# Forgetting attention with its query tiles in reverse order, the causal mask added to the key terms by GpSimd

## The chip, the cores and the metric

The kernel runs on one core of a Trainium2 chip. The metric is the device time of one execution in microseconds; lower is better. The engines are named TensorE (PE in the profile, its weight loads PEld), VectorE (DVE), ScalarE (ACT), GpSimd (POOL) and SyncE (SP).

## The reference, cut to what matters

Two transformer layers run one after the other over 1024 tokens (1040 with 16 meta tokens ahead). The first has a state-space part and a forgetting attention of 16 heads; the second has two more kinds of attention. Only the forgetting attention is touched:

```python
c = jnp.cumsum(logf, axis=1)                       # c: one value per token and head
...
s = jnp.einsum("bthd,bshd->bhts", qi, k).astype(jnp.float32) * scale
s = s + (cqi[..., :, None] - c_k[..., None, :])
s = jnp.where(kpos[None, :] <= qpos[:, None], s, -jnp.inf)
p = jax.nn.softmax(s, axis=-1).astype(v.dtype)
return jnp.einsum("bhts,bshd->bthd", p, v)
```

The term of the query in a row is the same for all keys and drops out of the softmax. The term of the key, and the mask, stay.

## The kernel before, in words

All instructions stand in the order in which the program issues them, and each engine works through its own in that order. The 16 heads go as eight pairs (p = 0 to 7; j = 0, 1 within a pair). For a pair, `fox_project` has made keys, queries and values in an earlier stretch, and `fox_attend` does the attention in eight query tiles of 128 rows, t = 0 to 7. The keys of tile t are the 16 meta columns and 128 (t + 1) more.

For each tile there are three steps. A: TensorE multiplies queries by keys (L566, L567: two products, since the operands are split in two parts), in one to three chunks of columns; the last chunk gets a third product (L569) of an identity with a table of 0 and 1e30 in bf16, which puts the mask into its last 128 columns. VectorE adds the key terms `cb`, takes the minimum (L570) and writes N. ScalarE takes the exponential in place (L573). GpSimd copies the 16 meta columns into `pm` (L576). B: TensorE transposes N in blocks of 128 columns (L624), up to four blocks to a PSUM bank, and ScalarE copies each bank to `pt` (L630). C: after every fourth tile, TensorE multiplies the group's transposed weights with the values (L604, and L607 for the meta columns), and VectorE scales the result (L609). The first group has tiles 0 to 3, the second tiles 4 to 7.

`pipeline` sets their order: A(0), A(1), then A(i + 2), C(i - 1), B(i) for each i. A, B and C return an estimate of their time, and `merge` weaves these steps with projections by such estimates: first with the gate's projection of this pair (two pieces of 24 products, L112 to L114, `fox_gate`), then, from the `None` that `pipeline` yields ahead of the last two tiles' transposes, with the projections for the next pair (keys in three pieces, then queries, then values). In the last pair these are strips of the convolution. When the gate's pieces are used up, attention goes on alone until that `None`. A key piece is taken out of PSUM by ScalarE and VectorE in turn, twice (`stack_q`, L443 and L444).

PSUM has eight banks of 512 columns, handed out in turn (`bank`); a product waits until the bank of eight ago has been read. Weights for projections are loaded by SyncE's queue and split in two by ScalarE (L120) and GpSimd (L121).

Of the kernel before, what the change touches and what calls it, by code (L numbers as in the profile page):

```python
# [9 lines left out]
F32 = mybir.dt.float32  # L10
F32R = mybir.dt.float32r
BF16 = mybir.dt.bfloat16
I32 = mybir.dt.int32
AF = mybir.ActivationFunctionType
ALU = mybir.AluOpType
# [51 lines left out]
class Kern:  # L67
# [128 lines left out]
    def consts(self):  # L196
        nc, V, cst = self.nc, self.nc.vector, self.cst
        self.w32 = cst.tile([128, 32], F32, name="w32")
        V.memset(self.w32, 0.0)
        V.memset(self.w32[0:64, 0:1], 1.0)  # L200
        V.memset(self.w32[64:128, 1:2], 1.0)
        V.memset(self.w32[:, 2:3], 1.0)
        self.identb = cst.tile([128, 128], BF16, name="identb")
        self.maskb = cst.tile([128, 128], BF16, name="maskb")
        V.tensor_copy(out=self.identb, in_=self.ident)
        V.tensor_copy(out=self.maskb, in_=self.cm[:, 3, :])
        self.ones = cst.tile([128, 128], F32, name="ones")
        V.memset(self.ones, 1.0)
        a, b = PARAM_COLS["conv_w"]
        self.cwh = cst.tile([128, 120], F32, name="cwh")  # L210
        V.tensor_scalar(out=self.cwh, in0=self.params[:, a:a + 120], scalar1=0.5, scalar2=None, op0=ALU.mult)
        self.gbh = cst.tile([128, 16], F32, name="gbh")
        V.tensor_scalar(out=self.gbh, in0=self.pslot("gate_bias"), scalar1=0.5, scalar2=None, op0=ALU.mult)
        self.sb48 = cst.tile([48, 1], F32, name="sb48")
        V.tensor_tensor(out=self.sb48, in0=self.pslot("b48")[:48], in1=self.pslot("sgn")[:48], op=ALU.mult)
# [322 lines left out]
    def fox_attend(self, p, st):  # L538
        nc, te = self.nc, self.nc.tensor
        cb = []  # L540
        for j in range(2):
            c = self.ph.tile([128, L], F32, tag="cb", name="cb", bufs=2)
            nc.sync.dma_start(out=c, in_=self.d_csp[2 * p + j].partition_broadcast(128))
            cb.append(c)
        vT = st.pop("vT")
        st["vm"] = self.v_meta(vT)
        st["v"] = self.v_tokens(vT, [16 + 128 * b for b in range(8)])
        y = self.slot("y", w=T)
        Ns, PTs, M = {}, {}, [None, None]

        def A(i):
            if i % 4 == 0:
                M[i // 4] = self.ph.tile([128, 2, 128], F32, tag="bt", name="pm", bufs=2)
            W = 16 + 128 * (i + 1)
            n = -(-W // 512)
            w = -(-W // (2 * n)) * 2
            Ns[i] = []
            for j in range(2):
                N = self.slot("N")
                mn = self.sm.tile([128, 3], F32, tag="mn", name="mn", bufs=4)  # L560
                qt = st["q"][j][:, i * 128:(i + 1) * 128]
                for c in range(n):
                    s0, s1 = c * w, min(W, c * w + w)
                    S = self.bank()[:, :s1 - s0]
                    last = c == n - 1
                    te.matmul(S, qt, st["k"][j][0][:, s0:s1], start=True, stop=False)  # L566
                    te.matmul(S, qt, st["k"][j][1][:, s0:s1], start=False, stop=not last)  # L567
                    if last:
                        te.matmul(S[:, s1 - s0 - 128:], self.identb, self.maskb, start=False, stop=True)  # L569
                    nc.vector.tensor_tensor_reduce(  # L570
                        out=N[:, s0:s1], in0=cb[j][:, s0:s1], in1=S, scale=1.0,
                        scalar=mn[:, c - 1:c] if c else HUGE, op0=ALU.add, op1=ALU.min, accum_out=mn[:, c:c + 1])
                nc.scalar.activation(out=N[:, :W], in_=N[:, :W], func=AF.Exp, scale=-1.0, bias=mn[:, n - 1:n],  # L573
                                     accum_out=self.lall[:, 2 * p + j, i:i + 1])
                c = 32 * (i % 4) + 16 * j
                nc.gpsimd.tensor_copy(out=M[i // 4][:, 0, c:c + 16], in_=N[:, 0:16])  # L576
                Ns[i].append(N)
            return 4 * max(W, 512) / 2.4

        def B(i):  # L580
            if i % 4 == 3:
                ps = self.bank()
                te.transpose(ps[:, :128], M[i // 4][:, 0], self.ident)
                nc.vector.tensor_copy(out=M[i // 4][:, 1], in_=ps[:, :128])
            if i % 4 == 0:

                PTs[i // 4] = [[self.ph.tile([128, 4, 512], F32, tag="pt", name="pt", bufs=4) for _ in range(2)]
                               for _ in range(i // 4 + 1)]
            q = slice((i % 4) * 128, (i % 4 + 1) * 128)
            for j in range(2):  # L590
                self.transposes(Ns[i][j], 16, i + 1, [pt[j][:, :, q] for pt in PTs[i // 4]], act=True)
            del Ns[i]
            return 2 * (i + 1) * 109

        def C(i):
            if i % 4 != 3:
                return 0
            g = i // 4
            pt = PTs.pop(g)
            O = self.bank()  # L600
            for b in range(i + 1):
                c0 = max(0, b - 4 * g) * 128
                for j in range(2):
                    te.matmul(O[64 * j:64 * j + 64, c0:], st["v"][:, b, 64 * j:64 * j + 64],  # L604
                              pt[b // 4][j][:, b % 4, c0:], start=b == 0, stop=False)
            for t in range(4):
                te.matmul(O[:, t * 128:(t + 1) * 128], st["vm"][:, t], M[g][:, 1], start=False, stop=t == 3)  # L607
            c = slice((i - 3) * 128, (i + 1) * 128)
            nc.vector.scalar_tensor_tensor(out=y[:, c], in0=O, scalar=0.5, in1=st["zs"][:, c], op0=ALU.mult,  # L609
                                           op1=ALU.mult)  # L610
            return (2.5 + 4 * g) * 910

        yield from self.pipeline(8, A, B, C)
        nc.sync.dma_start(out=self.d_yatt[p], in_=y)

# [1198 lines left out]
```

## Time and profile before

| | |
|---|---|
| time, median of 3 runs | 2726.68 us (2726.24 to 2726.96) |
| time of the profiled execution | 2726.84 us |
| span in the profile | 2725.1 us |
| busy share of the span: TensorE, VectorE, ScalarE, GpSimd | 98%, 49%, 43%, 27% |
| attention stage touched by the change | from 76 to some 670 us, eight pairs |

The span is the stretch of one execution that the profiler saw; times in the trace count from its start. A busy share is an average over many stages. Matmuls are pipelined and their ends are modelled, so the spacing from start to start says what a product costs, not its duration.

### The profile page before, as it was taken

The numbers are of one execution on the slowest core, as the hardware profiler recorded it, in microseconds if no ns is written. First come the engines' busy times: TensorE is split into PE (matmuls) and PEld (weight loads), VectorE is DVE, ScalarE is ACT, GpSimd is POOL, SyncE is SP. The second block draws the span as 40 slices with busy tenths as digits, with TensorE's granted clock in tenths as the row PEclk, the third lists the DMA queues.
The fourth block names the chain that finished last, engine by engine and source line by source line (L and its number), as shares of the span: only waits on it lengthen the run. The fifth ranks groups of instructions, "written<-read, shape, count | busy, mean of one in ns | idle before, by whom it ended". The sixth has DMA issues, their size and how long they took to land. (4 is left out here: it accounts for less than half of the span.)

```text
span 2725.1 us, 38660 instructions
## 1 busy us (share of the span) xinstructions
PE 2658.2 (98%) x14925; PEld 2229.8 (82%) x14925; DVE 1332.5 (49%) x2625; ACT 1165.5 (43%) x2080; POOL 729.7 (27%) x924
## 2 busy tenths in 40 slices
PE   8999999999999999999999999999999999998999
PEld 6888888888989889889877887878878877787877
DVE  5433322233574573654756777444644454346332
ACT  5554444444443433433432113445544454445331
POOL 1112122111253342342432334111121222225321
PEclk9999999999999999999999999999999999999999
DMA  3222222221123123122168654340222223325412
GB/s 126 64 61 75 78 74 75 78 58 68 39 87 116 55 78 115 55 92 103 55 192 282 207 174 149 108 134 23 85 63 78 79 74 107 95 72 155 155 62 70
DMA packets 85463, 266.86 MB, mean 98 GB/s; under 512 B 10880, under 2 KB 12032, under 8 KB 84256
## 3 DMA queue, kind: packets, MB, share of 16 engines
q1 hardware_dynamic: 81936, 255.68, 28.7%
q10 hardware_dynamic: 3344, 8.72, 1.5%
q8 instruction: 117, 1.92, 0.3%
q14 instruction: 66, 0.54, 0.1%
HBM read 205.57 MB, written 33.49 MB: 88 GB/s over the span
## 5 line engine op out<-in xcount | busy, mean ns | idle before, releaser
L121 POOL TENSOR_TENSOR wlo<-wraw,whi 128x1024 fp32r<-128x1024 f32 (+2 forms) x168 | 376.7, 2246 | 1064.9 <-ACT whi L120 857.6
L112 PE MATMUL bank<-uh,whi 128*128 128x512 f32 (+4 forms) x1752 | 626.6, 358 | 0.1
L114 PE MATMUL bank<-uh,wlo 128*128 128x512 f32 (+4 forms) x1752 | 619.3, 353 | 0.7 <-POOL wlo L121 0.7
L113 PE MATMUL bank<-ul,whi 128*128 128x512 f32 (+4 forms) x1752 | 619.2, 353 | 0.0
L114 PEld LDWEIGHTS bank<-uh,wlo 128*128 128x128 f32 (+1 forms) x1752 | 328.2, 187 | 36.1 <-POOL wlo L121 1.1
L112 PEld LDWEIGHTS bank<-uh,whi 128*128 128x128 f32 (+1 forms) x1752 | 328.5, 188 | 34.2 <-issue 1.1
L113 PEld LDWEIGHTS bank<-ul,whi 128*128 128x128 f32 (+1 forms) x1752 | 328.5, 187 | 32.3
L112 PE MATMUL bank<-u,whi 128*128 128x512 f32 x512 | 208.0, 406 | 0.7 <-ACT pr L935 0.7
L113 PE MATMUL bank<-u,whi 128*128 128x512 f32 x512 | 203.6, 398 | 0.0
L114 PE MATMUL bank<-u,wlo 128*128 128x512 f32 x512 | 203.2, 397 | 0.0
L120 ACT ACTIVATE whi<-wraw 128x1024 fp32r<-128x1024 f32 (+2 forms) x169 | 155.1, 926 | 17.8 <-DMA wraw<-in_w_pa_dram 13.8
L630 ACT ACTIVATE pt<-bank 128x512 f32<-128x512 f32 (+1 forms) x320 | 142.2, 508 | 40.7 <-PE bank L624 37.8
L114 PE MATMUL bank<-yh,wlo 128*128 128x512 f32 x384 | 153.1, 399 | 2.0 <-POOL wlo L121 1.8
L112 PE MATMUL bank<-yh,whi 128*128 128x512 f32 x384 | 152.9, 398 | 1.2 <-ACT whi L120 1.2
L113 PE MATMUL bank<-yl,whi 128*128 128x512 f32 x384 | 152.2, 396 | 0.0
L647 DVE SCALAR_TENSOR_TENSOR acc<-raw,cwh,acc 128x1040 f32<-128x1040 f32 x72 | 93.7, 1302 | 109.5 <-ACT acc L644 107.8
L573 ACT ACTIVATE N<-N,mn 128x272 f32<-128x272 f32 (+7 forms) x128 | 100.3, 786 | 45.6 <-DVE mn L570 44.7
L121 POOL TENSOR_TENSOR wo<-wl,wo 128x512 fp32r<-128x512 f32 x52 | 74.0, 1436 | 158.2 <-ACT wo L120 151.3
L114 PEld LDWEIGHTS bank<-u,wlo 128*128 128x128 f32 x512 | 97.4, 190 | 23.2
L112 PEld LDWEIGHTS bank<-u,whi 128*128 128x128 f32 x512 | 97.6, 191 | 22.2 <-ACT pr L935 1.1
L113 PEld LDWEIGHTS bank<-u,whi 128*128 128x128 f32 x512 | 97.6, 191 | 20.6
L624 PE MATMUL bank<-cm,N 128*128 128x128 f32 x832 | 106.9, 273 | 0.0
(326 smaller groups left out, 4954.6 us busy)
## 6 DMA issues: line engine op xcount, KB each, us to landing
wraw<-in_w_in_dram SPq DMA_DIRECT2D x120, 512.0 KB, 4.0
gt<-d_gate SPq DMA_DIRECT2D x48, 512.0 KB, 4.6
ab<-d_acs SPq DMA_DIRECT2D x32, 512.0 KB, 3.7
qs<-qt SPq DMA_DIRECT2D x48, 256.0 KB, 3.0
wl<-in_w_out_dram SPq DMA_DIRECT2D x48, 256.0 KB, 5.3
tab<-in_tab_dram SPq DMA_DIRECT2D x8, 1056.0 KB, 5.3
cb<-d_csp SPq DMA_DIRECT2D x16, 520.0 KB, 7.7
d_gate<-gt SPq DMA_DIRECT2D x16, 512.0 KB, 2.9
```

Source lines behind the costliest of these rows:

```text
L112: te.matmul(ps, lh, rh, start=start, stop=False)
L113: te.matmul(ps, lh, rl, start=False, stop=False)
L114: te.matmul(ps, ll, rh, start=False, stop=stop)
L120: self.nc.scalar.activation(out=hi, in_=src, func=AF.Copy)
L121: (self.nc.vector if vector else self.nc.gpsimd).tensor_tensor(out=lo, in0=src, in1=hi.bitcast(F32), op=ALU.subtract)
L573: nc.scalar.activation(out=N[:, :W], in_=N[:, :W], func=AF.Exp, scale=-1.0, bias=mn[:, n - 1:n], accum_out=self.lall[:, 2 * p + j, i:i + 1])
L624: nc.tensor.transpose(ps[:, b * 128:(b + 1) * 128], N[:, c:c + 128], self.ident)
L630: self.nc.scalar.activation(out=out, in_=ps, func=AF.Copy)
L647: V.scalar_tensor_tensor(out=acc[:, :L], in0=raw[:, k:k + L], scalar=w(k), in1=acc[:, :L], op0=ALU.mult, op1=ALU.add)
```

## The change

The mask product and its two bf16 tables go. The tile order is reversed: i still counts 0 to 7, and the tile is t = 7 - i. Before the first tile and after each tile's reduction, GpSimd adds the mask in place into the 128 columns of `cb` that lie on the diagonal of the next tile. Smaller tiles never read those columns, so each block of `cb` is masked once, when its tile is next. GpSimd's copies of the meta columns move behind both heads' exponentials. The groups come in the order tiles 7 to 4, then tiles 3 to 0.

```diff
-        self.identb = cst.tile([128, 128], BF16, name="identb")
-        self.maskb = cst.tile([128, 128], BF16, name="maskb")
-        V.tensor_copy(out=self.identb, in_=self.ident)
-        V.tensor_copy(out=self.maskb, in_=self.cm[:, 3, :])
...
+        def mask(j, t):
+            c = cb[j][:, 16 + 128 * t:144 + 128 * t]
+            nc.gpsimd.tensor_tensor(out=c, in0=c, in1=self.cm[:, 3], op=ALU.add)
+
+        mask(0, 7)
+        mask(1, 7)
+
         def A(i):
+            t = 7 - i
...
-                    te.matmul(S, qt, st["k"][j][1][:, s0:s1], start=False, stop=not last)
-                    if last:
-                        te.matmul(S[:, s1 - s0 - 128:], self.identb, self.maskb, start=False, stop=True)
+                    te.matmul(S, qt, st["k"][j][1][:, s0:s1], start=False, stop=True)
                     nc.vector.tensor_tensor_reduce(
                         out=N[:, s0:s1], in0=cb[j][:, s0:s1], in1=S, scale=1.0,
                         scalar=mn[:, c - 1:c] if c else HUGE, op0=ALU.add, op1=ALU.min, accum_out=mn[:, c:c + 1])
+                if t:
+                    mask(j, t - 1)
                 nc.scalar.activation(out=N[:, :W], in_=N[:, :W], func=AF.Exp, scale=-1.0, bias=mn[:, n - 1:n],
-                                     accum_out=self.lall[:, 2 * p + j, i:i + 1])
-                c = 32 * (i % 4) + 16 * j
-                nc.gpsimd.tensor_copy(out=M[i // 4][:, 0, c:c + 16], in_=N[:, 0:16])
+                                     accum_out=self.lall[:, 2 * p + j, t:t + 1])
                 Ns[i].append(N)
+            for j in range(2):
+                c = 32 * (t % 4) + 16 * j
+                nc.gpsimd.tensor_copy(out=M[t // 4][:, 0, c:c + 16], in_=Ns[i][j][:, 0:16])
             return 4 * max(W, 512) / 2.4
...
-            return 2 * (i + 1) * 109
+            return 2 * (t + 1) * 109
...
         def C(i):
             if i % 4 != 3:
                 return 0
-            g = i // 4
+            g = (7 - i) // 4
```

In the new numbering the score products are L571 and L572, the reduction L573, the exponential L578, the mask L551, the meta copy L583, the transposes L632, their copies L638, and the group's products L612 and L615. The order of three places in the fourth pair shows what moves.

On TensorE, the score products of tile 3 (528 key columns, two chunks of 264 for each head), before:

```order
L566 MATMUL bank<-kx_2621,qs_2771 128x264
L567 MATMUL bank<-ky_2622,qs_2771 128x264
L566 MATMUL bank<-kx_2621,qs_2771 128x264
L567 MATMUL bank<-ky_2622,qs_2771 128x264
L569 LDWEIGHTS identb
L569 MATMUL bank<-maskb,identb 128x128
L566 MATMUL bank<-kx_2623,qs_2773 128x264
```

The same place now, with the transposes of tile 5 behind it (12 blocks):

```order
L571 MATMUL bank<-kx_2657,qs_2789 128x264
L572 MATMUL bank<-ky_2658,qs_2789 128x264
L571 MATMUL bank<-kx_2657,qs_2789 128x264
L572 MATMUL bank<-ky_2658,qs_2789 128x264
L571 MATMUL bank<-kx_2659,qs_2791 128x264
L572 MATMUL bank<-ky_2660,qs_2791 128x264
L571 MATMUL bank<-kx_2659,qs_2791 128x264
L572 MATMUL bank<-ky_2660,qs_2791 128x264
L632 MATMUL bank<-cm,N_3077 128x128 x6
L632 MATMUL bank<-cm,N_3089 128x128 x6
```

The mask and its weight load are gone, so the second head's products follow the first head's directly.

On ScalarE, from the gate's second piece (its tanh, L519) to the first group's last copies, before:

```order
L519 ACTIVATE zs_3003<-bank 128x512
L630 ACTIVATE pt<-bank 128x2x128 x2
L573 ACTIVATE N_3143,lall<-N_3143,mn 128x656
L573 ACTIVATE N_3156,lall<-N_3156,mn 128x656
L630 ACTIVATE pt<-bank 128x3x128 x2
L573 ACTIVATE N_3179,lall<-N_3179,mn 128x784
L573 ACTIVATE N_3192,lall<-N_3192,mn 128x784
L630 ACTIVATE pt<-bank 128x4x128 x2
```

The same stretch now (its tanh is L515):

```order
L515 ACTIVATE zs_3017<-bank 128x512
L638 ACTIVATE pt<-bank 128x4x128 x4
L578 ACTIVATE N_3158,lall<-N_3158,mn 128x656
L578 ACTIVATE N_3170,lall<-N_3170,mn 128x656
...
L638 ACTIVATE pt<-bank 128x2x128
L578 ACTIVATE N_3253,lall<-N_3253,mn 128x400
L578 ACTIVATE N_3261,lall<-N_3261,mn 128x400
L638 ACTIVATE pt<-bank 128x4x128
L638 ACTIVATE pt<-bank 128x128
L638 ACTIVATE pt<-bank 128x4x128
L638 ACTIVATE pt<-bank 128x128
```

Between the gate's tanh and the first group's last copy there were two tiles' exponentials and the copies of three tiles; now there are three tiles' exponentials and the copies of four tiles, and these are the large ones.

On TensorE, around the second group's product, now (`vtok` are the values; L632 are the transposes of tiles 1 and 0, L591 that of the meta columns):

```order
L114 MATMUL bank<-uh_8_95,wlo_3019 128x348
L632 MATMUL bank<-cm,N_3292 128x128 x2
L632 MATMUL bank<-cm,N_3300 128x128 x2
L591 MATMUL bank<-cm,pm 128x128
L632 MATMUL bank<-cm,N_3346 128x128
L632 MATMUL bank<-cm,N_3353 128x128
L612 MATMUL bank<-pt,vtok_2966 64x512 x2
```

Before, a whole projection piece stood between the last tile's transposes and the second group's product, and another between the last two tiles' transposes; now the second group, which is the small one, follows its last transposes directly.

## Rows read from the trace of the kernel before

**Rows 1.** The page's first part: busy time, share of the span and instructions.
```profile
PE 2658.2 (98%) x14925; PEld 2229.8 (82%) x14925; DVE 1332.5 (49%) x2625; ACT 1165.5 (43%) x2080; POOL 729.7 (27%) x924
```

**Rows 2.** TensorE's waits from 60 to 690 us: total, times, longest, in us.
```profile
PE bank L604 <- ACT pt L630: 5.6, 8, 0.8
```

**Rows 3.** Windows of the fourth pair: length, then each engine's busy time and count.
```profile
309.95:386.60 76.65, 75.89 (x466) 64.62 (x464) 23.09 (x72) 35.61 (x80) 14.42 (x29) 1.00 0.24 69
324.89:341.04 16.15, 15.39 (x111) 12.79 (x109) 10.50 (x36) 10.70 (x24) 1.18 (x6) 1.00 0.09 32
316.21:319.26 3.05, 3.05 (x26) 2.48 (x24) 2.16 (x8) 1.68 (x6) 0.20 (x1) 1.00 0.01 3
325.24:326.73 1.49, 1.49 (x13) 1.27 (x12) 1.02 (x2) 0.99 (x3) 0.00 (x0) 1.00 0.00 0
```

**Rows 4.** Timeline of TensorE at two masks: start, duration, line and operation.
```profile
318.61 0.23 PE L569 MATMUL bank<-maskb,identb 128*128 128x128 bf16 x1
318.65 0.37 PE L566 MATMUL bank<-kx,qs 128*128 128x264 f32 x1
318.86 0.28 PE L567 MATMUL bank<-ky,qs 128*128 128x264 f32 x1
318.98 0.28 PE L566 MATMUL bank<-kx,qs 128*128 128x264 f32 x1
319.09 0.28 PE L567 MATMUL bank<-ky,qs 128*128 128x264 f32 x1
...
326.67 0.23 PE L569 MATMUL bank<-maskb,identb 128*128 128x128 bf16 x1
326.73 0.83 PE L624 MATMUL bank<-cm,N 128*128 128x128 f32 x6
```

**Rows 5.** Timeline of TensorE at eight transposes and at the first group's product.
```profile
329.13 1.04 PE L624 MATMUL bank<-cm,N 128*128 128x128 f32 x8
329.96 0.47 PE L566 MATMUL bank<-kx,qs 128*128 128x456 f32 x1
...
332.83 2.86 PE L604 MATMUL bank<-pt,vtok 128*64 128x512 f32 x16 [0.76 <-ACT pt L630]
```

**Rows 6.** Timeline of ScalarE in the same stretch.
```profile
319.21 0.61 ACT L573 ACTIVATE N<-N,mn 128x400 f32<-128x400 f32 x1
...
320.75 0.73 ACT L573 ACTIVATE N<-N,mn 128x528 f32<-128x528 f32 x1
...
325.08 0.60 ACT L519 ACTIVATE zs<-bank 128x512 f32<-128x512 f32 x1 [2.68 <-PE bank L114]
325.58 0.66 ACT L630 ACTIVATE pt<-bank 128x256 f32<-128x256 f32 x2
327.62 0.85 ACT L573 ACTIVATE N<-N,mn 128x656 f32<-128x656 f32 x1 [1.39 <-DVE mn L570]
...
328.75 0.84 ACT L573 ACTIVATE N<-N,mn 128x656 f32<-128x656 f32 x1 [0.18 <-DVE mn L570]
...
329.59 0.85 ACT L630 ACTIVATE pt<-bank 128x384 f32<-128x384 f32 x2
...
332.20 1.07 ACT L630 ACTIVATE pt<-bank 128x512 f32<-128x512 f32 x2
333.15 1.06 ACT L573 ACTIVATE N<-N,mn 128x912 f32<-128x912 f32 x1
```

**Rows 7.** Timeline of TensorE and ScalarE behind the second key piece.
```profile
348.80 0.93 PE L624 MATMUL bank<-cm,N 128*128 128x128 f32 x7
...
349.00 0.45 ACT L443 ACTIVATE kx<-bank 64x348 fp32r<-64x348 f32 x1 [1.52 <-PE bank L114]
350.03 0.46 ACT L443 ACTIVATE kx<-bank 64x348 fp32r<-64x348 f32 x1 [0.58 <-DVE ky L444]
350.51 1.85 ACT L630 ACTIVATE pt<-bank 128x512 f32<-128x512 f32 x4
```

**Rows 8.** A GpSimd group (busy, mean ns, idle before), and VectorE at a pair's start.
```profile
L761 POOL TENSOR_TENSOR yq<-yq,th 128x128 f32<-128x128 f32 x128 | 60.7, 506 | 126.5 <-DVE yq L758 126.5
...
311.35 0.30 DVE L570 CUSTOM_DVE_ANT_0 N<-cb,bank 128x144 f32<-128x144 f32 x1 [0.54 <-DMA cb<-d_csp]
```

More of the change, by code (lines that the diff above doesn't have):

```diff
@@ L549, in fox_attend @@
         Ns, PTs, M = {}, {}, [None, None]
+        def mask(j, t):
[3 more added lines that the diff above has]
+        mask(1, 7)
         def A(i):
+            t = 7 - i
             if i % 4 == 0:
-                M[i // 4] = self.ph.tile([128, 2, 128], F32, tag="bt", name="pm", bufs=2)
-            W = 16 + 128 * (i + 1)
+                M[t // 4] = self.ph.tile([128, 2, 128], F32, tag="bt", name="pm", bufs=2)
+            W = 16 + 128 * (t + 1)
             n = -(-W // 512)
@@ L560, in A @@
                 mn = self.sm.tile([128, 3], F32, tag="mn", name="mn", bufs=4)
-                qt = st["q"][j][:, i * 128:(i + 1) * 128]
+                qt = st["q"][j][:, t * 128:(t + 1) * 128]
                 for c in range(n):
@@ L564, in A @@
                     S = self.bank()[:, :s1 - s0]
-                    last = c == n - 1
                     te.matmul(S, qt, st["k"][j][0][:, s0:s1], start=True, stop=False)
-                    te.matmul(S, qt, st["k"][j][1][:, s0:s1], start=False, stop=not last)
-                    if last:
-                        te.matmul(S[:, s1 - s0 - 128:], self.identb, self.maskb, start=False, stop=True)
+                    te.matmul(S, qt, st["k"][j][1][:, s0:s1], start=False, stop=True)
                     nc.vector.tensor_tensor_reduce(
@@ L572, in A @@
                         scalar=mn[:, c - 1:c] if c else HUGE, op0=ALU.add, op1=ALU.min, accum_out=mn[:, c:c + 1])
+                if t:
+                    mask(j, t - 1)
                 nc.scalar.activation(out=N[:, :W], in_=N[:, :W], func=AF.Exp, scale=-1.0, bias=mn[:, n - 1:n],
-                                     accum_out=self.lall[:, 2 * p + j, i:i + 1])
-                c = 32 * (i % 4) + 16 * j
-                nc.gpsimd.tensor_copy(out=M[i // 4][:, 0, c:c + 16], in_=N[:, 0:16])
+                                     accum_out=self.lall[:, 2 * p + j, t:t + 1])
                 Ns[i].append(N)
+            for j in range(2):
+                c = 32 * (t % 4) + 16 * j
+                nc.gpsimd.tensor_copy(out=M[t // 4][:, 0, c:c + 16], in_=Ns[i][j][:, 0:16])
             return 4 * max(W, 512) / 2.4
         def B(i):
+            t = 7 - i
+            g = t // 4
             if i % 4 == 3:
                 ps = self.bank()
-                te.transpose(ps[:, :128], M[i // 4][:, 0], self.ident)
-                nc.vector.tensor_copy(out=M[i // 4][:, 1], in_=ps[:, :128])
+                te.transpose(ps[:, :128], M[g][:, 0], self.ident)
+                nc.vector.tensor_copy(out=M[g][:, 1], in_=ps[:, :128])
             if i % 4 == 0:
-                PTs[i // 4] = [[self.ph.tile([128, 4, 512], F32, tag="pt", name="pt", bufs=4) for _ in range(2)]
-                               for _ in range(i // 4 + 1)]
-            q = slice((i % 4) * 128, (i % 4 + 1) * 128)
+                PTs[g] = [[self.ph.tile([128, 4, 512], F32, tag="pt", name="pt", bufs=4) for _ in range(2)]
+                          for _ in range(g + 1)]
+            q = slice((t % 4) * 128, (t % 4 + 1) * 128)
             for j in range(2):
-                self.transposes(Ns[i][j], 16, i + 1, [pt[j][:, :, q] for pt in PTs[i // 4]], act=True)
+                self.transposes(Ns[i][j], 16, t + 1, [pt[j][:, :, q] for pt in PTs[g]], act=True)
             del Ns[i]
-            return 2 * (i + 1) * 109
+            return 2 * (t + 1) * 109
         def C(i):
@@ L597, in C @@
                 return 0
-            g = i // 4
+            g = (7 - i) // 4
             pt = PTs.pop(g)
             O = self.bank()
-            for b in range(i + 1):
+            for b in range(4 * g + 4):
                 c0 = max(0, b - 4 * g) * 128
@@ L607, in C @@
                 te.matmul(O[:, t * 128:(t + 1) * 128], st["vm"][:, t], M[g][:, 1], start=False, stop=t == 3)
-            c = slice((i - 3) * 128, (i + 1) * 128)
+            c = slice(512 * g, 512 * g + 512)
             nc.vector.scalar_tensor_tensor(out=y[:, c], in0=O, scalar=0.5, in1=st["zs"][:, c], op0=ALU.mult,
```

## The prediction

> **What bounds the kernel now.** The page comes first: TensorE is busy for 98% of the span, so a change pays only through TensorE's own work or through its waits [rows 1]. The table of waits of the attention stage (its eight head pairs) has one entry that matters: products of weights and values (L604) wait 5.6 us in eight pieces for ScalarE's copies of transposed weights [rows 2]. The windows view takes one pair: TensorE is busy 75.89 of 76.65 us, ScalarE 35.61, GpSimd 14.42 [rows 3]. The 0.76 us left over is that one wait [rows 5]. The other row is what to watch: in the 16.15 us in which TensorE does attention work alone, with no projection between, ScalarE is busy 10.70 us, two thirds of the time, where it is under half busy over the pair [rows 3]. So the question is what the new order puts into that stretch.
>
> **Mask products removed.** All 128 go (16 in each pair). TensorE's timeline gives the price from start to start [rows 4]: the next product starts 0.04 us after the mask, but then takes 0.21 us until its successor starts, where the same shape without a mask ahead takes 0.11 to 0.13. So a mask followed by a product of that format costs 0.04 + 0.09 = 0.13 us. One followed by transposes costs 0.06 (326.67 to 326.73). In each pair 11 are of the first sort (the eight of j = 0 and three of j = 1) and 5 of the second: 11 x 0.13 + 5 x 0.06 = 1.73 us, 13.8 us for eight pairs. The same 0.09 us is paid at each change from transposes or group products back to a projection; the order has four of these in a pair before and two now: 2 x 0.09 x 8 = 1.4 us more. Gain: 15.2 us. Its bounds: 0.04 x 128 = 5 us, if the slow successor is not the mask's doing, and 0.13 x 128 + 1.4 = 18 us; I stay near the upper end, since the successor is slow in each row behind a mask and in none behind its own kind. The two casts at the start of the program go too; they lie on VectorE, and I count nothing for them (below 1 us).
> The Trainium skill (TensorE: Matmul & The Clock Gate, Back-to-back issue gap) gives about 81 ns for a product of 128 columns with its weight load in a sustained stream. By that figure 128 masks would be 10.4 us, and the forecast 3 us later; the rows' spacing is used here.
>
> **The masks on GpSimd.** 128 additions of 128x128 are new; the same operation and shape stands elsewhere in the program at 506 ns [rows 8]. That is 8.1 us more in a pair, on an engine busy 14.42 of 76.65. Each is issued right after the reduction of the tile before, and VectorE needs it only for the last columns of the next tile, after another tile's transposes. Ahead of it in GpSimd's queue stand the 16-column copies of a tile whose exponentials are done by then. At a pair's start the key terms' transfer lands late (VectorE waits 0.54 us for it now [rows 8]) and two masks follow it; the gate's projection covers that, some 5.6 us on TensorE (its second piece lies from 319.26 to 324.89 in the windows [rows 3]). I take zero. If the covers fail, the price is 0.5 us for each mask that ScalarE then waits for.
>
> **The first group's wait.** The order of the query tiles decides what is left when the gate's projection has run out. Before, that stretch begins with the third small tile's transposes; now it begins with the largest. I add up both engines from the end of the gate's second piece (t = 0) to the first group's product.
> TensorE: the transposes of tiles 7, 6, 5, 4 are 16 + 14 + 12 + 10 at 0.83/8 = 0.104 us [rows 5], 5.4 us, with one for the meta columns 5.5. The score products of tiles 1, 2, 3 and 4 take 3.05 + 1.49 us in the trace [rows 3]; without the two transposes among them (0.2) and their eight masks (4 x 0.13 + 4 x 0.06), and with the one change of format more, they come to 3.7. TensorE could start at 9.2 us.
> ScalarE, whose queue is in program order, must first do [rows 6]: the gate's tanh (done 0.7 us after the piece ends, 325.08 + 0.5 against the transposes' start at 324.89 us); four copies of 512 columns (0.48 each: from 332.20 to 333.15 for two): 2.6 us. Then tile 4's exponentials (656 wide): its products start at 1.7, and in the trace the exponential comes 2.4 us after them, of which VectorE spent some 0.4 on the gate; with 2.0 it starts at 3.7, and the second is 1.1 us later and 0.84 long: 5.6 us. Then tile 6's copies (2 x (0.48 + 0.37)): 7.3; tile 3's exponentials (2 x 0.73): 8.8; tile 5's copies (2 x (0.48 + 0.28), the tail of 0.12 of a pair's last one taken off): 10.3; tile 2's exponentials (2 x 0.61): 11.5; tile 4's copies up to the second head's first (0.48, half of 0.28, 0.48): 12.6 us, and about 0.1 until it has landed.
> So TensorE is held from 9.2 to 12.7, less some 0.5 us for the first head's product, which needs only the first copy: 3.0 us in place of 0.76 [rows 5]. PSUM's eight banks spread this wait over transposes and scores of the stretch, which doesn't change its sum. Cost: 8 x 2.2 = 17.6 us. Bounds of the wait: 1.7 us, if tile 4's exponentials need not be waited for, and 4.0, if masks hold VectorE back (a rival below).
>
> **The second group's wait.** Before, the order had a whole projection piece between its tiles' last transposes and its product. Now tile 1's and tile 0's transposes stand directly ahead of it. The piece before them ends at the transposes' start, 348.80 us in the trace; ScalarE takes the key copies first, the second of them only after VectorE's part of the first, and comes to the transposes' copies at 350.51, 1.7 us later [rows 7]. Copies of 256, 256 and 128 columns bring it to 2.5 us for the first head; TensorE has done its seven transposes at 7 x 0.104 = 0.73. Wait: 1.8 us in seven pairs. In the eighth the piece is a convolution strip's with a single copy: 0.7. Sum 13.3 us; before, zero. Bounds: 0.8 us a pair, if the second key copy went ahead of its wait, and 1.9.
> What is late next: nothing. Only projections follow in each pair, and their weights are split earlier; TensorE runs through them unheld now.
>
> **The sum.** -15.2 + 17.6 + 13.3 = +15.7 us. The profiled execution took 2726.84 us (span 2725.1), 0.16 above the median of the three runs, 2726.68. Forecast: 2742 us, 0.6% slower.
>
> **Rivals.** What a measurement of this kernel can tell from no change is about 0.2%: 2721.2 to 2732.1 us.
> (1) ScalarE keeps pace, faster. If its queue reached the last copy by 10 us in place of 12.7, the first wait would stay 0.76, and with the second one absent too the time is 2726.8 - 15.2 = 2712 us. For it: over the pair ScalarE is not half busy [rows 3]. Against it: the durations in the stretch are rows, and before the change the wait was there with a lighter queue. It decides from the point where both waits together are under 0.76 + 15.2/8 = 2.7 us in a pair; I add up 4.8. Chance 0.12.
> (2) Only one of the waits appears. With the first alone, 17.6 - 15.2 = +2: 2729 us. With the second alone, 13.3 - 15.2 = -2: 2725 us. For it: TensorE's queue may take up a short wait as slack; the 1.8 us rests on a single spacing. Against it: in-order copies leave nothing to start on. No measurable change. Chance 0.16.
> (3) The masks hold VectorE. Each addition on GpSimd delays the reduction beside it by 0.5 us; two of these are ahead of tile 4's second exponential, for which ScalarE idles anyway: 1.0 us a pair, +8: 2750 us. For it: both engines work on the same key terms. Against it: later delays are hidden, as ScalarE has a backlog from there on. Chance 0.12.
> The Trainium skill (SBUF — State Buffer, Who interferes with whom) says that VectorE is held by a GpSimd instruction that reads SBUF when it has two SBUF inputs, and not with one at most; this reduction reads key terms from SBUF and scores from PSUM, so by that rule (3) would not come from the memory's port. No row here shows it either way.
> (4) The forecast, both waits as summed: 0.60.
>
> **How the numbers follow.** Slower by over 0.2% holds (4), (3) and a little of (2): 0.74. Same holds most of (2): 0.15. Faster is (1) less its edge: 0.11. The range must leave out at most 2 in 10: below, it takes in the first-wait case of (2) at 2729 and stops ahead of (1); above, it takes in (3) with the second wait at its bound, 2756. So 2728 to 2756; for (4) alone 2733 to 2751.
>
> **What would show it.** Right: no L569; TensorE's busy time in the stage down by some 15 us; waits of the group products for ScalarE's copies up from 5.6 us to over 25, in two places of each pair; a pair's period up from 76.65 to some 78.6 us; ScalarE without a gap from tile 4's exponentials to tile 4's copies; GpSimd some 60 us busier with nobody waiting for it. Wrong: waits of VectorE for GpSimd's masks, a period under 76, or group products that start without a wait.

## The result and the profile after

The changed kernel took 2748.63 us (median of five runs, 2744.37 to 2752.05) beside 2726.68 us of the kernel before on the same chip: ratio 1.0082, 95% interval 1.0068 to 1.0096, so 0.8% slower. The forecast was 2742 us within 2728 to 2756. The profiled execution took 2744.37 us (span 2742.3), 17.5 us above that of before (2726.84), where the sum said 15.7.

The page of the changed kernel, part 1:

```profile
PE 2649.9 (97%) x14797; PEld 2241.7 (82%) x14797; DVE 1335.5 (49%) x2623; ACT 1168.3 (43%) x2080; POOL 784.7 (29%) x1052
```

TensorE has 128 products fewer and is busy 8.3 us less than in [rows 1]; GpSimd is busy 55 us more. So TensorE does less and ends later: it waits. The table of its waits from 60 to 700 us answers to [rows 2] (waiting line, what it waits for: total, times, longest):

```profile
PE bank L612 <- ACT pt L638: 26.8, 16, 1.9
PE bank L571 <- DVE zs L516: 2.2, 1, 2.2
PE bank L632 <- DVE mn L573: 1.5, 8, 0.4
...
PE bank L112 <- DVE mn L573: 1.1, 1, 1.1
```

The wait of the group products for ScalarE's copies has gone from 5.6 us in eight pieces to 26.8 in sixteen, two in each pair. Below it stand eight short waits of transposes for VectorE, one in each pair, and two single ones in the first pair, none of which the prediction had. The first pair had one such wait before the change as well, which [rows 2] does not show:

```profile
PE bank L566 <- DVE mn L570: 1.4, 1, 1.4
```

The windows view takes each pair from its first transpose of the values to the next pair's. Here are the first, second and fourth pair, with two stretches of the first pair behind them (length, busy time and count of TensorE, its weight loads, VectorE, ScalarE and GpSimd, then the granted clock, as a share of 2.4 GHz, and the DMA):

```profile
76.59:162.91 86.32, 79.28 (x454) 68.85 (x453) 30.97 (x87) 36.27 (x82) 21.80 (x46) 0.96 0.26 78
162.91:242.72 79.81, 75.98 (x456) 67.02 (x455) 23.44 (x72) 36.83 (x81) 21.02 (x45) 1.00 0.22 64
321.62:400.41 78.79, 75.01 (x448) 66.33 (x447) 23.35 (x72) 35.88 (x79) 21.35 (x45) 1.00 0.24 67
88.00:92.00 4.00, 1.02 (x2) 0.50 (x2) 2.75 (x4) 1.34 (x3) 2.44 (x2) 0.75 0.00 0
92.00:96.00 4.00, 3.88 (x9) 3.14 (x10) 3.48 (x13) 2.56 (x5) 1.45 (x5) 0.50 0.00 0
```

Before, the same three pairs are 79.13, 77.45 and 76.62 us long. The fourth pair, which stands for the steady state, has grown by 2.17 us: TensorE is busy 0.9 us less than in [rows 3] and idle 3.78 us in place of 0.76. The first pair has grown by 7.2 us, and in it the granted clock falls to the lower level, 1.2 GHz (0.50 from 92 to 96 us), after 4 us in which TensorE was busy for 1.02. From the eighth pair to the end the profiled run is 3.9 us shorter than that of before, most of which is not the change's: the run of before had a stretch at the lower clock near 1440 us, up to 3.4 us of work (0.79, 0.50 and 0.86 in three windows of 4 us from 1436 us), and this one has none there. The other four runs are 4 to 8 us longer than the profiled one; their mean granted clocks are 0.993 to 0.995, and 0.996 in the profiled one. An experiment below shows a place where the clock falls.

TensorE's timeline in the fourth pair at the two group products, with the start of the stretch (338.55) and of the last transposes (367.58):

```profile
338.55 1.91 PE L632 MATMUL bank<-cm,N 128*128 128x128 f32 x16
...
348.44 0.28 PE L572 MATMUL bank<-ky,qs 128*128 128x272 f32 x1
350.59 6.45 PE L612 MATMUL bank<-pt,vtok 128*64 128x512 f32 x32 [1.87 <-ACT pt L638]
356.98 1.16 PE L615 MATMUL bank<-pm,vm 128*128 128x128 f32 x8
...
367.58 0.60 PE L632 MATMUL bank<-cm,N 128*128 128x128 f32 x4
...
370.18 2.54 PE L612 MATMUL bank<-pt,vtok 128*64 128x512 f32 x16 [1.67 <-ACT pt L638]
```

ScalarE's timeline in the same stretch:

```profile
338.75 0.60 ACT L515 ACTIVATE zs<-bank 128x512 f32<-128x512 f32 x1 [0.81 <-PE bank L114]
339.24 2.06 ACT L638 ACTIVATE pt<-bank 128x512 f32<-128x512 f32 x4
342.07 0.84 ACT L578 ACTIVATE N<-N,mn 128x656 f32<-128x656 f32 x1 [0.77 <-DVE mn L573]
...
343.23 0.85 ACT L578 ACTIVATE N<-N,mn 128x656 f32<-128x656 f32 x1 [0.22 <-DVE mn L573]
...
344.07 1.82 ACT L638 ACTIVATE pt<-bank 128x512 f32<-128x512 f32 x4
...
349.91 1.45 ACT L638 ACTIVATE pt<-bank 128x512 f32<-128x512 f32 x4
```

Read against the prediction's clock, which starts where the gate's piece ends (338.55): tile 4's exponentials start at 3.5 (forecast 3.7), tile 4's copies at 11.4 (11.5), the first group's product at 12.0 (12.2). From 344.07 on ScalarE has no recorded gap. In the second group the product starts 2.6 us after the last transposes begin (2.5).

The first pair, on all engines (the softplus chain of the state-space part, L334 to L337, is VectorE's work from before; L120 splits a weight):

```profile
77.67 3.57 DVE L334 SCALAR_TENSOR_TENSOR dt<-dt,dt 128x288 f32<-128x288 f32 x7
...
82.58 0.51 DVE L573 CUSTOM_DVE_ANT_0 N<-cb,bank 128x348 f32<-128x348 f32 x1
...
87.70 1.04 ACT L120 ACTIVATE whi<-wraw 128x1024 fp32r<-128x1024 f32 x1
...
88.64 0.57 ACT L515 ACTIVATE zs<-bank 128x512 f32<-128x512 f32 x1
...
89.25 0.69 DVE L516 SCALAR_TENSOR_TENSOR zs<-zs,bank 128x512 f32<-128x512 f32 x1 [2.75 <-ACT zs L515]
...
90.00 0.70 PE L571 MATMUL bank<-kx,qs 128*128 128x392 f32 x1 [2.17 <-DVE zs L516]
...
92.12 0.80 PE L112 MATMUL bank<-uh,whi 128*128 128x512 f32 x1 [1.10 <-DVE mn L573]
```

Tile 7's scores stand from 77.38 us, but VectorE is at its chain until 82.58. Then six reductions follow (before, two short ones stood there), so the exponentials are late, the gate's tanh behind them is late, VectorE waits 2.75 us for the tanh, and the last scores of tile 5 (two chunks of 392 columns for each head) start 2.17 us late, as no bank of PSUM is free.

### The profile page after: what moved, and what is told of

Same layout as the page of the kernel before. It is cut to its first block, busy times and chain, and to the rows that moved or that the text cites. A ratio compares the mean times of both kernels' runs of the same rounds, so it can differ in the third digit from the quotient of the medians.

```text
span 2742.3 us, 38458 instructions
## 1 busy us (share of the span) xinstructions
PE 2649.9 (97%) x14797; PEld 2241.7 (82%) x14797; DVE 1335.5 (49%) x2623; ACT 1168.3 (43%) x2080; POOL 784.7 (29%) x1052
## 5 line engine op out<-in xcount | busy, mean ns | idle before, releaser
L638 ACT ACTIVATE pt<-bank 128x512 f32<-128x512 f32 (+1 forms) x320 | 142.0, 517 | 76.2 <-PE bank L632 73.4
L120 ACT ACTIVATE whi<-wraw 128x1024 fp32r<-128x1024 f32 (+2 forms) x169 | 154.9, 924 | 27.5 <-DMA wraw<-in_w_pa_dram 14.3
L578 ACT ACTIVATE N<-N,mn 128x912 f32<-128x912 f32 (+7 forms) x128 | 101.6, 806 | 54.4 <-DVE mn L573 53.5
L632 PE MATMUL bank<-cm,N 128*128 128x128 f32 x832 | 111.1, 275 | 2.2 <-DVE mn L573 1.5
```

What stands on the lines that cost most here:

```text
L120: self.nc.scalar.activation(out=hi, in_=src, func=AF.Copy)
L632: nc.tensor.transpose(ps[:, b * 128:(b + 1) * 128], N[:, c:c + 128], self.ident)
L638: self.nc.scalar.activation(out=out, in_=ps, func=AF.Copy)
```

## The experiments

All medians against the kernel before on the same chip, with the length of the first and the fourth pair (from values to values, from each profile) and the granted clock of the runs:

| run | us | ratio, 95% interval | first pair | fourth pair | clock |
|---|---|---|---|---|---|
| before | 2726.68 to 2728.38 | | 79.13 | 76.62 | 0.994 to 0.997 |
| changed | 2748.63 | 1.0082, 1.0068 to 1.0096 | 86.32 | 78.79 | 0.993 to 0.996 |
| order alone | 2753.56 | 1.0092, 1.0079 to 1.0105 | 83.86 | 79.72 | 0.993 to 0.997 |
| forward, no mask | 2723.52 | 0.9986, 0.9977 to 0.9995 | 78.97 | 76.04 | 0.994 to 0.996 |
| reverse, no mask | 2750.30 | 1.0078, 1.0066 to 1.0090 | 85.96 | 78.80 | 0.993 to 0.996 |
| second group later | 2740.08 | 1.0037, 1.0023 to 1.0051 | 84.36 | 76.94 | 0.992 to 0.996 |
| gate's piece later | 2764.83 | 1.0135, 1.0121 to 1.0148 | 86.14 | 80.76 | 0.992 to 0.996 |
| chain later | 2749.99 | 1.0083, 1.0069 to 1.0097 | 81.87 | 78.72 | 0.994 to 0.996 |
| all three | 2752.98 | 1.0091, 1.0077 to 1.0105 | 81.92 | 78.82 | 0.992 to 0.994 |
| before, gate and chain later | 2724.62 | 0.9990, 0.9982 to 0.9999 | 78.47 | 76.02 | 0.993 to 0.997 |
| copies on VectorE | 2737.62 | 1.0035, 1.0022 to 1.0048 | 84.86 | 77.41 | 0.993 to 0.995 |
| three mended | 2713.35 | 0.9949, 0.9937 to 0.9962 | 75.50 | 75.54 | 0.996 to 0.997 |
| before, mended | 2720.15 | 0.9968, 0.9957 to 0.9979 | 75.95 | 76.02 | 0.994 to 0.997 |
| six copies | 2716.18 | 0.9958, 0.9945 to 0.9972 | 75.32 | 75.35 | 0.995 to 0.997 |

Medians of runs on different chips are compared by their ratios. The pairs' lengths are the sharper measure: the fourth pair of each profiled run lies clear of stretches at the lower clock (1.00 in all of them).

**What the masks cost: order alone.** The changed kernel with the mask products back and no addition on GpSimd:

```diff
-te.matmul(S, qt, st["k"][j][1][:, s0:s1], start=False, stop=True)
+te.matmul(S, qt, st["k"][j][1][:, s0:s1], start=False, stop=not last)
+if last:
+    te.matmul(S[:, s1 - s0 - 128:], self.identb, self.maskb, start=False, stop=True)
...
-mask(j, t - 1)
```

> The new tile order with the 128 mask products kept on TensorE and no additions on GpSimd. Theory (two waits of TensorE for ScalarE): the masks of tiles 4 to 1 (8 in a pair, 0.76 us) fall into a stretch in which TensorE is held anyway, so only the other 0.97 us of the pair's 1.73 come back on top of the changed kernel: 2748.6 + 8 x 0.97 = 2756 us. Rival (the masks cost their full price wherever they stand): 2748.6 + 13.8 = 2762 us. Rival (the additions on GpSimd are what made the changed kernel slow): below 2748 us.

Measured: the fourth pair is 79.72 us, 0.93 above the changed kernel's 78.79 (0.97 expected); the median is 4.9 us above the changed kernel's rather than 7.8 (2.7 by the two ratios). The first pair is 2.5 us shorter here: its two single waits come to 2.5 us in place of 3.3, and the granted clock stays at 1.00, where it is 0.96 in the changed kernel. The order alone costs 3.10 us a pair, and the removed products give back 0.93 of the 1.73 that their price adds up to: those in the held stretch are free.

**Forward, no mask.** The kernel before without the causal mask:

```diff
-if last:
-    te.matmul(S[:, s1 - s0 - 128:], self.identb, self.maskb, start=False, stop=True)
```

> The kernel before, in its own order, with the causal mask left out altogether (the outputs of the upper triangle are thereby part of the softmax). Theory: 13.8 us less for the mask products, of which the two tiles in the stretch ahead of the first group's product (0.38 us a pair, 3.0 in all) go into its wait for ScalarE: 2726.7 - 13.8 + 3.0 = 2716 us, and that wait up from 5.6 to some 8.6 us. Rival (a mask costs only the 0.04 us to its successor's start): 2726.7 - 5 = 2722 us. By the skill page's 81 ns: 2726.7 - 10.4 + 3 = 2719 us.

Measured: 0.58 us a pair and 4.5 us by the median, far less than expected. The wait at the product rose to 7.5 us in all (8.6 expected), and the time, 2723.5 us, lies nearest to the rival's 2722, but the price of a mask is not the rival's 0.04 us. TensorE's timeline of this run in the fourth pair, the same places as in [rows 3, 5]:

```profile
323.71 0.60 PE L622 MATMUL bank<-cm,N 128*128 128x128 f32 x4
...
325.92 0.43 PE L566 MATMUL bank<-kx,qs 128*128 128x392 f32 x1
...
327.43 0.27 PE L581 MATMUL bank<-cm,pm 128*128 128x128 f32 x1
327.54 1.13 PE L622 MATMUL bank<-cm,N 128*128 128x128 f32 x8
328.79 0.47 PE L566 MATMUL bank<-kx,qs 128*128 128x456 f32 x1
...
331.66 2.86 PE L602 MATMUL bank<-pt,vtok 128*64 128x512 f32 x16 [0.95 <-ACT pt L628]
```

And of the kernel before, at the scores of the same tile 5:

```profile
327.31 0.43 PE L566 MATMUL bank<-kx,qs 128*128 128x392 f32 x1
...
329.02 0.28 PE L583 MATMUL bank<-cm,pm 128*128 128x128 f32 x1
```

The tile takes 1.51 in place of 1.71 us: 0.10 us for a mask, as forecast (0.13 and 0.06 in turn). By the figure of the Trainium skill (TensorE: Matmul & The Clock Gate, Back-to-back issue gap), about 81 ns, the estimate would be 0.16 us for the two; the rows' price, 0.19, is nearer to the measured 0.20. But from the start of tile 1's transposes to the group product it is 7.95 us (323.71 to 331.66), and it was 7.94 with six masks in it (324.89 in [rows 3] to 332.83 in [rows 5]). The eight transposes of tile 3 now take 1.25 us from start to start, where they took 0.83 [rows 5], and the wait is longer, 0.95 after 0.76. So in the old order too ScalarE sets when the product starts, and the six masks ahead of it were free: of their 0.6 us, 0.42 went into slower transposes, without an entry in the table of waits. Of the other ten, the four of tiles 0 and 7 gave 0.35 us, about their price. The six of tiles 1 to 3 gave only 0.19, and three score products of tile 3 now take 0.18 to 0.23 us to their successor, where 0.12 is usual. They stand behind products of their own kind, so a slow successor is not the mask's alone, as the prediction had it; what holds them no run shows.

**Reverse, no mask.** The changed kernel without the additions on GpSimd, so again without the causal mask:

```diff
-mask(0, 7)
-mask(1, 7)
...
-if t:
-    mask(j, t - 1)
```

> The changed kernel with the causal mask left out: no additions on GpSimd, all else the same. Theory (the additions are hidden): 2747 to 2749 us, the steady period 78.8 us, both waits unchanged. Rival (the additions hold VectorE and through it ScalarE at tile 4's exponentials, 1.0 us a pair): 2740.6 us and a period of 77.8 us.

Measured: 78.80 us, the same to 0.01; the additions cost nothing. In the changed kernel VectorE does wait for them, a sign that the prediction had named for being wrong. Its waits from 60 to 700 us:

```profile
DVE N L573 <- POOL cb L551: 4.2, 24, 0.2
```

These are some three short waits in each pair, and the pair is as long without them. Reductions of 456 columns, by line and form on VectorE from 160 to 640 us, changed kernel and then this one:

```profile
L573 DVE CUSTOM_DVE_ANT_0 N<-cb,bank 128x456 f32<-128x456 f32 x12 | 7.5, 624 | 0.0
```

```profile
L570 DVE CUSTOM_DVE_ANT_0 N<-cb,bank 128x456 f32<-128x456 f32 x12 | 7.5, 624 | 0.0
```

624 ns with the additions beside them and without. The Trainium skill (SBUF — State Buffer, Who interferes with whom) says that a VectorE instruction with at most one input in SBUF does not contend with GpSimd; the trace agrees. The same profile shows what the wait can do to the clock. Windows in its fifth pair, around the first group's product (429.84, after a wait of 1.90 us):

```profile
428.00:430.00 2.00, 0.16 (x1) 0.17 (x2) 0.65 (x4) 2.00 (x8) 0.39 (x2) 1.00 0.67 238
430.00:432.00 2.00, 2.00 (x6) 0.96 (x7) 0.00 (x0) 1.60 (x6) 0.39 (x2) 0.63 0.06 25
432.00:434.00 2.00, 2.00 (x7) 1.00 (x6) 0.00 (x0) 0.00 (x0) 0.00 (x0) 0.51 0.00 0
```

TensorE was busy 0.16 of 2 us, then the granted clock is 0.63 and 0.51 for 4 us, and this pair is 80.57 us long in place of 78.80. It happened in two of the eight pairs of this run at this place, and in none of the changed kernel's profiled run.

**The second wait: second group later.** One projection piece between the last transposes and the product:

```diff
-return 2 * (t + 1) * 109
+return 2 * (t + 1) * 109 + (1500 if i == 7 else 0)
```

> The changed kernel with one projection piece between the last tile's transposes and the second group's product. Theory: 1.8 us less in seven pairs, 2748.6 - 12.6 = 2736 us, steady period 77.0 us, and TensorE's waits of group products for ScalarE's copies from 26.8 us to some 14. Rival (the wait only moves to what follows, as ScalarE's queue is no shorter): 2748 us and period 78.8.

Measured: 76.94 us, 1.85 less; the table of waits now reads

```profile
PE bank L612 <- ACT pt L638: 15.2, 9, 1.9
```

that is, seven waits are gone and nothing took their place. Two of the runs, at a clock of 0.995 and 0.996, took 2731.7 and 2732.9 us, the other four 2738 to 2742 us at 0.992 and 0.993.

**The first wait: gate's piece later.** The first merge's ratio puts the gate's second piece behind the transposes of tiles 7 and 6:

```diff
-merge(att, zipped(self.fox_gate(p, st), ssd_dt), 1.5, stop=True)
+merge(att, zipped(self.fox_gate(p, st), ssd_dt), 0.63, stop=True)
```

> The changed kernel with the gate's second piece issued later: behind the transposes of tiles 7 and 6 in place of ahead of them, so that ScalarE's copies and exponentials of the first four tiles have a cover on TensorE. Theory (the first wait is ScalarE's backlog at the end of the gate's projection): TensorE's wait at the first group's product falls from 1.9 us to under 1, the steady period from 78.8 to some 77.2 us, the time by 10 to 14 us to 2735 to 2739. Rival (ScalarE's work between the key terms and the first group decides, wherever the piece stands): period 78.8, no change.

Measured: 80.76 us, 2.0 worse; both theories missed. ScalarE's timeline:

```profile
334.11 1.06 ACT L578 ACTIVATE N<-N,mn 128x912 f32<-128x912 f32 x1 [2.17 <-DVE mn L573]
...
346.26 0.60 ACT L515 ACTIVATE zs<-bank 128x512 f32<-128x512 f32 x1 [1.79 <-PE bank L114]
...
348.69 0.74 ACT L578 ACTIVATE N<-N,mn 128x528 f32<-128x528 f32 x1 [1.83 <-DVE mn L573]
```

ScalarE ran dry ahead of the piece, in it and behind it: tile 3's scores, which would have fed it, now stood behind the piece. A cover helps only while ScalarE has work queued; here it cut the supply. The product still waits 1.66 us.

**Copies on VectorE.** The second head's copies of tiles 5 and 4 leave ScalarE's queue:

```diff
-self.transposes(Ns[i][j], 16, t + 1, [pt[j][:, :, q] for pt in PTs[g]], act=True)
+self.transposes(Ns[i][j], 16, t + 1, [pt[j][:, :, q] for pt in PTs[g]], act=j == 0 or i not in (2, 3))
...
-if act or self.ev % 2:
+if act or act is None and self.ev % 2:
```

> The changed kernel with four copies of each pair (those of the second head of tiles 5 and 4, 1.4 us) taken from ScalarE's queue to VectorE. Theory (the first wait is the length of ScalarE's queue up to tile 4's copies): TensorE's wait at the first group's product falls from 1.9 to some 0.5 us, steady period from 78.8 to 77.4 us, time by 11 to 2737 us. Rival (VectorE's reductions pace that stretch, since ScalarE waits for them at each tile): the copies delay the reductions of tiles 3 and 2, period 78.8 or more.

Measured: 77.41 us and 2737.6 us, both as the theory had it, though the product's own wait is still 1.20 us (0.5 expected). The first group's product and the one behind it:

```profile
344.59 5.81 PE L612 MATMUL bank<-pt,vtok 128*64 128x512 f32 x32 [1.20 <-ACT pt L638]
350.33 1.16 PE L615 MATMUL bank<-pm,vm 128*128 128x128 f32 x8
```

The product starts 11.29 us after the stretch begins (at 333.30) in place of 12.04, and it takes 5.74 us from its start to the next line's in place of 6.39. So 0.75 us of the gain lie ahead of it and 0.65 in it: in the changed kernel it was held again on its way, for the second head's copies. The length of ScalarE's queue up to tile 4's copies is the cause of the first wait.

**The first pair: chain later.** The softplus steps and what hangs on them run beside the projection behind the first pair:

```diff
-self.softplus(sp[:, :, 0:32])
...
 def dt_ssd(self):
+    yield from self.softplus(self.sp[:, :, 0:32])
...
-merge(att, zipped(self.fox_gate(p, st), ssd_dt), 1.5, stop=True)
+merge(att, zipped(self.fox_gate(p, st), ssd_dt if p else iter(())), 1.5, stop=True)
...
-merge(att, self.fox_project(p + 1, nx), 2.5, lead=2000.0)
+merge(att, zipped(self.fox_project(p + 1, nx), iter(()) if p else ssd_dt), 2.5, lead=2000.0)
```

> The changed kernel with VectorE's softplus chain of the state-space part (nine us, ahead of the first pair's reductions) spread over the projection behind the first pair; the attention itself is unchanged. Theory (the first pair's extra 5 us are reductions that start late, and TensorE's lower clock after the wait): first pair's period from 86.3 to some 81 us, no fall of the granted clock at 90 us, time 5 us less, 2743 us; the steady period stays 78.8. Rival (the first pair is late because its key terms and masks are): 86 us as before.

Measured: the first pair fell from 86.32 to 81.87 us, with the granted clock at 1.00 throughout, but the second rose from 79.81 to 84.54, and the time stayed. VectorE's first reduction there is this,

```profile
163.41 0.52 DVE L573 CUSTOM_DVE_ANT_0 N<-cb,bank 128x348 f32<-128x348 f32 x1 [10.66 <-DMA cb<-d_csp]
```

and, in the table of waits of the DMA queue on SP from 140 to 166 us, what stood ahead of the key terms' transfer (L539):

```profile
SPq L421 <- ACT arow L419: 10.7, 1, 10.7
```

Tile 7's scores began at 158.35 us. The key terms landed late, since their transfer stood in SP's queue behind that of the moved part's result, which held the queue for 10.7 us; from there the same sequence followed, with a wait of 2.1 us for the gate and a granted clock of 0.73 behind it (172 to 176 us). So in two cases of different origin a late first reduction was enough. The old order pays for this one too: in the run "before, gate and chain later" the second pair rises by 3.4 us, here by 4.7.

**All three**, these edits together:

> The changed kernel with the three edits together: second group's product one projection piece later, gate's second piece inside the stretch, softplus chain later. Theory (the three costs are separate): steady period 78.8 - 1.9 - 1.6 = 75.3 us, first pair some 78, time 2748.6 - 12.6 - 12 - 5 = 2719 us, faster than the kernel before by 8. Rival (the waits share one cause, ScalarE's load, and one of them comes back): period 76.6 or more, time 2729 or more.

Measured: 78.82 us and 2752.98. By the single runs, 78.79 - 1.85 + 1.97 = 78.91: additive, with the gate's piece undoing what the second group's gave. The 2719 us of the theory are missed since the gate's piece was counted as a gain.

**Before, gate and chain later**, the same on the old order:

> The kernel before (its order, its mask products) with the same two edits that fit it: the gate's second piece later, the softplus chain later. It tells how much of the combined version's gain needs the new order and the masks on GpSimd. Theory: the wait of 0.76 us goes, steady period 75.9 us, first pair 77 in place of 79, time 2728 - 6 - 2 = 2720 us. Rival (its wait is not moved by the piece): 2726 us, the first pair alone.

Measured: 76.02 us, and the group products' wait is gone from the table; there the piece works as a cover. The second pair is 80.82 us, again by the moved part, so the time is 2724.6 and not 2720. The first group's product in this run (two lines), and in the kernel before the line behind the product that starts at 332.83 in [rows 5]:

```profile
335.30 2.38 PE L604 MATMUL bank<-pt,vtok 128*64 128x512 f32 x16
337.61 1.16 PE L607 MATMUL bank<-pm,vm 128*128 128x128 f32 x8
```

```profile
335.62 1.16 PE L607 MATMUL bank<-pm,vm 128*128 128x128 f32 x8
```

The same 16 products take 2.31 us here and 2.79 before the change. So TensorE was held for 0.48 us within the product, beside the recorded wait of 0.76: 1.24 us in all.

**Three mended**: second group later, copies on VectorE, and the softplus alone moved to the projection behind the first pair (what hangs on it now runs beside the gate's projection of the second pair):

> The changed kernel with the second group's product later, the four copies on VectorE, and the softplus chain alone (nothing behind it) moved to the projection behind the first pair. Theory (three separate costs): steady period 78.8 - 1.9 - 1.4 = 75.5 us, first pair some 78.5, second some 76.5, time 2748.6 - 12.6 - 11 - 4.5 = 2720.5 us, 0.2 to 0.3% faster than the kernel before. Rival (the copies on VectorE give nothing): period 76.9, 2731 us.

Measured: 2713.35 us, better than expected, 3.0 us of it by the first pair (78.5 expected). Its first, second and fourth pair:

```profile
76.30:151.80 75.50, 74.07 (x449) 63.89 (x448) 35.11 (x91) 35.31 (x77) 22.35 (x46) 1.00 0.29 89
151.80:228.67 76.87, 75.38 (x454) 64.75 (x453) 25.85 (x78) 35.01 (x78) 21.41 (x45) 1.00 0.24 69
305.16:380.70 75.54, 74.13 (x449) 63.89 (x448) 25.02 (x76) 34.49 (x75) 21.39 (x45) 1.00 0.24 70
```

The first pair is as short as the fourth, and in all five runs the granted clock is 0.996 or 0.997.

**Before, mended**: the gate's piece later and the softplus alone moved, on the old order with its mask products:

> The kernel before, in its order and with its mask products, with the gate's second piece later and the softplus chain alone moved. Theory: the second pair's 80.8 us of the run with the whole chain moved goes back to some 76.5, steady period 76.05, time 2724.6 - 4 = 2720.5 us: what the mended new order reaches is then to be had without it. Rival: 2724 us as there.

Measured: as expected, 2720.15 us. So more than half of the gain over the kernel before, 7.7 of 14.5 us, needs neither the new order nor GpSimd's masks. The two intervals overlap a little; the fourth pairs, 75.54 and 76.02, put 0.48 us a pair on the side of the new order.

**Six copies**: also the second head of tile 6.

```diff
-act=j == 0 or i not in (2, 3)
+act=j == 0 or i not in (1, 2, 3)
```

> The version with three mended places, and two more copies of each pair (the second head of tile 6, 0.84 us of ScalarE's queue) on VectorE. Theory (ScalarE's queue sets the first wait as long as VectorE has room): the wait at the first group's product falls from 1.2 us to some 0.4, steady period from 75.5 to 74.8 us, time 2713 - 5.5 = 2708 us. Rival (VectorE's reductions of tile 3 are delayed by the copies ahead of them, and ScalarE's exponentials with them): period 75.5 or more, 2713 us.

Measured: 75.35 us, only 0.19 less (the longest wait at a group product is 0.9 us, where 0.4 was expected), and the median is not below that of three mended. ScalarE's timeline shows the rival's sign:

```profile
330.49 0.74 ACT L578 ACTIVATE N<-N,mn 128x528 f32<-128x528 f32 x1 [0.35 <-DVE mn L573]
```

Tile 3's exponentials now wait for VectorE, where in three mended they stood without a gap. So four copies are about what VectorE has room for in this stretch.

## Why the prediction was right, and where it was short

- **Mask products removed, -15.2 us (1.9 a pair).** The price of one is right: 0.10 us in the run without masks. As time it came through only where TensorE is not held: 0.93 us a pair in the new order, 0.58 in the old. The sum allowed for that in the new order, since it took the longer wait from a TensorE without masks. TensorE's busy time fell by 8.3 us and not by some 15, as slowed products count as busy: the first group's takes 6.45 us in place of 5.81, and some of the first pair's ran at the lower clock.
- **Masks on GpSimd, 0.** Right: 78.80 and 78.79 us. Rival (3) is refuted, and VectorE's durations don't change. The 24 short waits of VectorE are a sign of being wrong that came true without a cost.
- **First group's wait, 3.0 us in place of 0.76.** The difference is right, and both sizes are low. TensorE reaches the product after 10.0 us of the stretch rather than 9.2, so 0.8 is spread over transposes, as said, and the product starts at 12.0: 2.8 us. Then 0.65 more are lost within the product: 3.5 in all. Before the change, it was 1.24. The difference is 2.26 us a pair, and 2.24 was forecast; that the two shortfalls of some 0.5 us cancel is luck.
- **Second group's wait, 1.8 us in seven pairs.** Right: 1.67 us at the product, 1.85 a pair when it is taken away. In the eighth pair it is 0.51 us (0.7 forecast).
- **The sum in the steady state.** -1.9 + 2.2 + 1.8 = +2.1 us a pair was forecast, +2.17 measured. Both waits are there, which refutes rivals (1) and (2). That the profiled run as a whole also came near the sum, 17.5 for 15.7 us, is partly luck: the first pair lost 5.0 us more than the steady state, and from the eighth pair to the end this run is 3.9 us the shorter one.
- **What fell short** is the sentence "What is late next: nothing", with the claim that the gate's projection covers the pair's start. In the first pair VectorE's chain ends 5.2 us after the scores begin, the cover does not hold, and the pair grows by 7.2 us in place of 2. The chain ran into this pair before the change too, but ahead of two short reductions, not six. The run with the chain moved took 4.45 us off it and the mended version the rest. The granted clock had no term at all: in the profiled run it falls in the first pair, and the other runs, 4 to 8 us longer, are those at 0.993 to 0.995. That it can fall behind the first group's wait is seen in two pairs of the reversed run without masks; where it fell in the changed kernel's other four runs no profile shows, so that part of the 22 us is argued, not shown.

## What to carry to other kernels

Work removed from the bounding engine pays only outside the stretches in which that engine is already held, and a held stretch shows in operations that run slower than their like (a group's product of 2.79 us in place of 2.31), not only in the table of waits. A new order of tiles must be costed on the engine that feeds the next stage, at the steady pair and again at the first one, where leftovers of the stage before still occupy it. Once the waits are found, a longer cover can cut the supply of the engine that it is to help; taking work off that engine's queue was the surer cure here, as far as the engine that took it had room.

## What the runs showed of the hardware

- A wait of 1.9 us of TensorE was followed by some 4 us at a granted clock of 0.51 to 0.63 in one pair and left it at full in others of the same program (two of eight pairs in the reversed run without masks); it cost 1.8 us. With waits of 1.2 us (three mended) the whole attention stage of the profiled run stayed at full clock, 2.4 GHz.
- Four copies out of PSUM (512 columns twice, 256 and 128) that took 1.40 us of ScalarE's busy time in a pair took 1.68 us of VectorE's, and the pair became 1.38 us shorter.
- Additions of 128x128 on GpSimd took 460 ns beside reductions of VectorE on the same tile, and left these at 624 ns.
